# First projections of an encoder layer: spills begun from ScalarE, rows of the first norm stored two tiles later, low parts of those weights on VectorE

## The chip, the core and the metric

The kernel runs on one core of one Trainium2 chip. The core has four compute engines with a queue of instructions each (TensorE, shown as PE; VectorE, DVE; ScalarE, ACT; GpSimd, POOL) and SyncE (SP), which here only starts DMAs. Each queue is worked off in order: an instruction that waits holds up all that stand behind it on its engine. The metric is the device time of one execution in microseconds (us).

## The reference

Two independent sequences of 512 tokens with 1024 features pass through one encoder layer, all in float32. Cut to what matters:

```python
def encoder_layer(x, p, ...):
    h = layer_norm(a * x + 0.5 * swiglu(x, ffn1_wg, ffn1_wu, ffn1_wd), ln1_g, ln1_b)
    proj = h @ w_in
    gq, gk, gv, gr, zf, zb, aq, ak, av = jnp.split(proj, offs, axis=-1)
    o_gla = gla_mixer(gq, gk, gv, gr, zf, zb, ...)   # chunked gated linear attention, both directions
    o_att = gqa_mixer(aq, ak, av, q_norm_g, k_norm_g) # 8 query heads, 2 key heads, 2-D rotary positions
    mix = jnp.concatenate([o_gla, o_att], axis=-1) @ w_out
    h = layer_norm(a * h + mix, ln2_g, ln2_b)
    h = layer_norm(a * h + 0.5 * swiglu(h, ffn2_wg, ffn2_wu, ffn2_wd), ln3_g, ln3_b)
    return h + jax.nn.sigmoid(h @ w_pg + b_pg) * (p @ w_pe)
```

The part of this text is `proj = h @ w_in` and what stands around it: the first norm before it, and attention after it.

## The kernel before

**Numbers in two parts.** TensorE multiplies operands of type fp32r. Each float32 operand is split into a high part, which ScalarE rounds off (line 137), and a low part, the difference, which another engine forms (line 138). Three products (high x high, high x low, low x high) are summed in PSUM. So each piece of weights passes DMA (`raw`, line 149), ScalarE (`w` high), VectorE or GpSimd (`w` low), TensorE. `piece` picks the engine of the low part; for the projections it is GpSimd. `raw` has three buffers, `w` six; a piece is 128x512 (128x288 for the group `akvz`), and a DMA brings two pieces.

**Stages.** Feed-forward layer 1 (0 to about 654 us), the projections and, woven among them, attention and gated linear attention (to about 1200 us), feed-forward layer 2, the gate at the end. This text speaks of the first 110 us of the second stage.

**The first projections.** `projections()` runs groups of matmuls one behind the other: `akvz(0)` (keys, values and decay inputs of sequence 0), `aq(0)` (queries), `g_gr(0)` and `g_gr(1)` (the swish gate of both sequences), then the same for sequence 1, `g_gv` and `g_gqk`. A group (`tok_group`) holds four PSUM banks `pm`, one for each 128 tokens; four steps of two pieces of weights go through all four banks. One tick is three matmuls, a group 32 ticks. A bank is free again when its result is read: ScalarE reads `gr` with Silu into an `ev` buffer (line 757), and since it is needed much later, it is spilled to DRAM (`put`, line 752). `ev` has three buffers, so the fourth result of a group needs the first spill to have landed.

**Side work at ticks.** `main.weave(h1_rows(0), ...)` and its like set side work between ticks: the transposes of the normed rows (`flip`, line 658, in `h1T`), the rows themselves (`h1_rows`: gain and bias on VectorE, lines 650 and 651, then a store `sp_h` of the row tile, 128x1024), and at tick 102 `qk_stacks`, which transposes keys and queries of sequence 0 (line 879, ScalarE lines 884 and 889, VectorE lines 886 and 890). At tick 130 attention begins (line 909 is its first product). The rotary step works on VectorE and GpSimd in turns (lines 807, 812, 814, 815).

**What sets the order.** TensorE's order is the order in which the code is written. The queues of the other engines are ordered by the scheduler of the framework when the program is built. All DMAs go through SP's queue: weights, row stores and spills in one line.

The lines that the change touches, at their places in the listing: `put` (751), `g_gr` (754), `g_gv` (765), `g_gqk` (772), `prefetch` (160), `h1_rows` (1215) and its two weaves (1224, 1226).

Of the kernel before, what the change touches and what calls it, by code (L numbers as in the profile page):

```python
# [20 lines left out]
NT = 4  # L21
# [49 lines left out]
class Layer:  # L71
    def __init__(self, tc, ctx, d, outs):
        self.tc, self.nc, self.d, self.outs = tc, tc.nc, d, outs
        P = lambda name, bufs, **k: ctx.enter_context(tc.tile_pool(name=name, bufs=bufs, **k))
        self.cp = P("const", 1)
        self.xp = P("x", 4)
        self.yp = P("y", 8)
        self.wp = P("w", 6)
        self.rp = P("raw", 3)
        self.rx, self.turn = None, 0  # L80
        self.sp = P("small", 4)
        self.pm = P("pm", 4, space=bass.MemoryType.PSUM)
        self.pd = P("pd", 4, space=bass.MemoryType.PSUM)
        self.X = {}
        self.Y = {}
        self.table = None
        self.queue, self.raws, self.ready = [], [], []
        self.todo, self.W, self.D, self.XB, self.st = [], {}, {}, [], {}

    def const(self, name, shape, dt=F32):  # L90
# [69 lines left out]
    def prefetch(self):  # L160
        while len(self.ready) < 4 and (self.raws or self.queue):
            r = self.raws.pop(0) if self.raws else self.raw(self.queue.pop(0))
            n = r.shape[1] // 2
            self.ready += [self.piece(r[:, :n]), self.piece(r[:, n:])]
        while len(self.raws) < 2 and self.queue:
            self.raws.append(self.raw(self.queue.pop(0)))

# [59 lines left out]
    def load_x(self, X):  # L227
# [20 lines left out]
        def s1(c):  # L248
            sub(raw[0, c], raw[0, c], raw[1, c])
            nc.vector.tensor_tensor(raw[1, c], raw[1, c], raw[1, 2 + c], ALU.add)  # L250
            put(raw[1, c], 4, c)

        def s2(c):
            sub(raw[1, c], raw[1, 2 + c], raw[0, c])
            put(raw[1, c], 5, c)
# [467 lines left out]
class Middle:  # L723
# [24 lines left out]
    def ev(self, name):  # L748
        return self.ep.tile([128, 512], F32, tag="ev", name=name)

    def put(self, n, s, t, tl):
        self.nc.sync.dma_start(self.spill[n, s][t], tl)

    def g_gr(self, s):
        def evac(t, b):
            g = self.ev("gr")
            self.nc.scalar.activation(g, b, AF.Silu)  # L757
            self.put("G", s, t, g)
        return self.L.tok_group(s, 4, 512, 0, evac)

    def preload(self):
# [3 lines left out]
    def g_gv(self, s):  # L765
        def evac(t, b):
            g = self.ev("gv")
            self.nc.scalar.activation(g, b, AF.Copy)
            self.put("gv", s, t, g)
        return self.L.tok_group(s, 4, 512, 0, evac)  # L770

    def g_gqk(self, s):
        nc, L = self.nc, self.L
        for u in range(4):
            w = [L.next_w().rearrange("p h (k f) -> p h k f", k=4) for _ in range(2)]
            p = L.bank_m()
            for kt in range(NKT):
                x = L.X[s][kt // 4][:, kt % 4]
                for m, (a, b) in enumerate(((0, 0), (0, 1), (1, 0))):
                    nc.tensor.matmul(p, w[kt // 4][:, a, kt % 4], x[:, b], start=(kt == 0 and m == 0),  # L780
                                     stop=(kt == NKT - 1 and m == 2))
                if kt == NKT - 1:
                    g = self.ev("gqk")
                    nc.scalar.activation(g, p, AF.Copy, scale=0.125 if u < 2 else 1.0)
                    self.put("gqk", s, u, g)
                yield

    def rms(self, ss, n, div, eps, tag):
# [363 lines left out]
def build(tc, d, outs):  # L1152
    nc = tc.nc
    ctx = ExitStack()
    with ctx:
        L = Layer(tc, ctx, d, outs)
# [10 lines left out]
        h1, z2 = dram("h1"), dram("z2")  # L1167
# [16 lines left out]
        def mid(hp):  # L1184
            L.ident = L.const("ident", (128, 128))
            L.consts(hp)
        with tc.tile_pool(name="rx1", bufs=3, reuse_waits="tile") as L.rx:
            ffn = Ticker(L.ffn(1, lambda s, t: d["x"][s, t * 128:(t + 1) * 128, :], ln_tail(1, L.rx), mid=mid))
            first = L.flip(0, 1, "h1T")
            ffn.put(first, [tail + n for n in (19, 22, 25, 28)])  # L1190
            ffn.end()
        with ExitStack() as mctx:
            M = Middle(L, mctx, h1)
# [16 lines left out]
            main = Ticker(projections())  # L1210
            lnr = M.m8("lnr", (128, 2, 1024))
# [1 line left out]
                L.row(1, j, lnr[:, j])  # L1213

            def h1_rows(s):
                for t in range(NT):
                    L.affine(L.Y[s, t], lnr[:, 0], lnr[:, 1])
                    M.put("h1", s, t, L.Y[s, t])
                    yield
            main.place(first, (1, 5, 9, 13))  # L1220
            main.to(32)
            for _ in L.later:
                pass
            main.weave(h1_rows(0), 4, 48)
            main.weave(L.flip(1, 1, "h1T"), 8, 84)
            main.weave(h1_rows(1), 4, 100)

            main.to(PLAN["s0"])
            main.weave(M.qk_stacks(0, q0, o0[0], (None, 0, 1, 2, 3)), 5, PLAN["s1"])
            main.to(130)  # L1230
            M.preload()
# [56 lines left out]
            main = Ticker(M.wout(1, 0))  # L1288
# [22 lines left out]
        with ExitStack() as fctx:  # L1311
# [38 lines left out]
            main = Ticker(finish())  # L1350
# [93 lines left out]
```

## Time and profile before

| | before |
|---|---|
| median of three runs | 1956.47 us (1953.67 to 1960.98) |
| profiled execution, its own time | 1953.48 us |
| its span, first to last instruction | 1951.7 us |
| TensorE busy | 1877.6 us (96%) |
| VectorE busy | 1413.1 us (72%) |
| ScalarE busy | 873.8 us (45%) |
| GpSimd busy | 860.5 us (44%) |
| mean granted TensorE clock | 0.985 |

The span is what the profile covers; 1.8 us of the execution lie around it. The shares are averages over four stages, so they tell little of one stretch of 110 us: for it the views are asked with a window. In rows of the timeline the first number is the start, the second the time from the first start to the last end of the instructions merged in the row; what stands in brackets is the idle time of the engine before them and what ended it. In rows of waits stand the sum, the count and the longest. In a windows row stand, after the stretch and its length, the busy time (and count) of PE, PEld (weight loads), DVE, ACT and POOL, the granted TensorE clock (1.00 is full speed), the DMA engines' share and GB/s.

### The profile page before, as it was taken

Reading aid. Unit: us, or ns where it says so; the run is one execution under the profiler, and the core shown is the slowest. Engines: PE = TensorE matmul, PEld = TensorE weight load, DVE = VectorE, ACT = ScalarE, POOL = GpSimd, SP = SyncE. Lnnn points to the kernel's source line nnn. Section 1 sums busy time; section 2 is a strip of 40 time slices with the busy share of each in tenths; the row PEclk is TensorE's granted clock in tenths of the full one; section 3 lists DMA queues with packets and bytes.
Section 4 is the critical chain, followed back from the end, with each engine's and each line's share of the span. In section 5 each row is a group of like instructions: output and inputs, shape, how many; then the busy total and the mean of one; then the engine's idle time right before and its main releaser. Section 6 shows DMA issues by size and latency. Waiting matters only on the chain. (4 is left out here: it accounts for less than half of the span.)

```text
span 1951.7 us, 25305 instructions
## 1 busy us (share of the span) xinstructions
PE 1877.6 (96%) x8838; PEld 1535.1 (79%) x8838; DVE 1413.1 (72%) x2143; ACT 873.8 (45%) x1654; POOL 860.5 (44%) x644
## 2 busy tenths in 40 slices
PE   7999999999999898989998898999999999999999
PEld 5788888888888777777876667888888888888787
DVE  7856566666886985788777879556566659895973
ACT  5445544444231355757752437445444442231342
POOL 0665565561550362342233343665565552451243
PEclk9999999999999998999998998999999999999999
DMA  4425443478865224222443231434443479766232
GB/s 180 162 103 173 169 150 144 158 279 343 316 252 195 91 72 156 84 82 92 140 152 87 87 119 55 161 114 158 173 161 141 162 274 338 297 256 247 76 122 84
DMA packets 104959, 322.22 MB, mean 165 GB/s; under 512 B 11008, under 2 KB 38400, under 8 KB 99456
## 3 DMA queue, kind: packets, MB, share of 16 engines
q1 hardware_dynamic: 104832, 320.61, 45.7%
q8 instruction: 70, 1.15, 0.2%
q14 instruction: 57, 0.47, 0.1%
HBM read 218.85 MB, written 101.71 MB: 164 GB/s over the span
## 5 line engine op out<-in xcount | busy, mean ns | idle before, releaser
L138 POOL TENSOR_TENSOR w<-raw,w 128x512 fp32r<-128x512 f32 (+1 forms) x318 | 431.8, 1367 | 750.3 <-ACT w L137 685.6
L137 ACT ACTIVATE w<-raw 128x512 fp32r<-128x512 f32 (+1 forms) x586 | 363.4, 624 | 449.2 <-POOL raw L269 85.8
L269 POOL TENSOR_TENSOR raw<-raw 128x512 f32<-128x512 f32 x240 | 355.9, 1491 | 227.4 <-DVE w L138 155.6
L425 PE MATMUL pm<-X,w 128*128 128x512 f32 x1848 | 434.6, 393 | 10.9 <-ACT X L137 7.8
L425 PEld LDWEIGHTS pm<-X,w 128*128 128x128 f32 x1848 | 347.2, 188 | 89.7 <-ACT X L137 8.6
L138 DVE TENSOR_TENSOR w<-raw,w 128x512 fp32r<-128x512 f32 x268 | 263.2, 990 | 115.5 <-ACT w L137 111.6
L425 PE MATMUL pd<-X,w 128*128 128x512 f32 x1320 | 307.9, 391 | 2.9 <-DVE w L138 2.2
L425 PEld LDWEIGHTS pd<-X,w 128*128 128x128 f32 x1320 | 247.5, 188 | 57.8 <-DVE w L138 3.0
L539 PE MATMUL pm<-w,XB 128*128 128x512 f32 x864 | 198.4, 389 | 0.8 <-DVE Y L523 0.8
L715 PE MATMUL pm<-w,h1T 128*128 128x512 f32 (+1 forms) x768 | 185.6, 384 | 14.0 <-ACT gr L757 9.9
L539 PEld LDWEIGHTS pm<-w,XB 128*128 128x128 f32 x864 | 162.0, 188 | 35.2 <-DVE Y L523 1.7
L138 DVE TENSOR_TENSOR hs<-sg,hs 128x512 fp32r<-128x512 f32 (+1 forms) x182 | 145.4, 818 | 49.6 <-ACT hs L137 48.4
L137 ACT ACTIVATE hs<-sg 128x512 fp32r<-128x512 f32 (+1 forms) x182 | 98.4, 561 | 166.1 <-DVE sg L391 64.8
L715 PEld LDWEIGHTS pm<-w,h1T 128*128 128x128 f32 x768 | 136.3, 195 | 36.5 <-ACT gr L757 10.1
L539 PE MATMUL pd<-w,XB 128*128 128x512 f32 x648 | 148.8, 389 | 0.0
L539 PEld LDWEIGHTS pd<-w,XB 128*128 128x128 f32 x648 | 121.6, 188 | 25.2
L523 DVE TENSOR_TENSOR Y<-Y,pm 128x512 f32<-128x512 f32 x104 | 70.4, 682 | 36.1 <-PE pm L539 36.0
L371 DVE TENSOR_TENSOR sg<-u,pm 128x512 f32<-128x512 f32 x22 | 15.1, 687 | 107.7 <-PE pm L425 107.7
L715 PE MATMUL pm<-w,h3T 128*128 128x512 f32 x384 | 90.6, 393 | 0.0
L715 PEld LDWEIGHTS pm<-w,h3T 128*128 128x128 f32 x384 | 71.2, 188 | 14.7 <-DVE h3T L670 0.2
L660 ACT ACTIVATE pd<-pd,c_lnT 128x512 f32<-128x512 f32 x48 | 36.0, 751 | 92.6 <-PE pd L658 92.6
L523 DVE TENSOR_TENSOR Y<-Y,pd 128x512 f32<-128x512 f32 x88 | 58.7, 678 | 19.3 <-PE pd L539 19.3
(237 smaller groups left out, 2542.1 us busy)
## 6 DMA issues: line engine op xcount, KB each, us to landing
hs<-hs SPq DMA_DIRECT2D x126, 512.0 KB, 2.6
XB<-hs SPq DMA_DIRECT2D x42, 1536.0 KB, 7.0
raw<-in_wgu SPq DMA_DIRECT2D x88, 512.0 KB, 3.4
raw<-in_wd SPq DMA_DIRECT2D x36, 512.0 KB, 7.2
hs_t<-hs SPq DMA_DIRECT2D x56, 256.0 KB, 2.5
XB<-hs_t SPq DMA_DIRECT2D x26, 512.0 KB, 5.1
raw<-in_wout SPq DMA_DIRECT2D x16, 512.0 KB, 3.6
raw<-in_wpg SPq DMA_DIRECT2D x16, 512.0 KB, 3.5
```

Source lines behind the costliest of these rows:

```text
L137: first = nc.scalar.activation(hi, raw, AF.Copy)
L138: (eng or nc.vector).tensor_tensor(lo, raw, hi.bitcast(F32), ALU.subtract)
L269: (sums or self.nc.gpsimd).tensor_tensor(o(), x(), y(), ALU.subtract)
L371: add = lambda o, x, y: nc.vector.tensor_tensor(o, x, y, ALU.add)
L425: nc.tensor.matmul(bank, w[:, a, kt * 128:(kt + 1) * 128], X[k][:, kt, b], start=(k in (0, 1, 4) and kt == 0 and m == 0), stop=(kt == 3 an ...
L523: nc.vector.tensor_tensor(yv, yv, bank, ALU.add)
L539: nc.tensor.matmul(b[t], h[:, a, t * 128:(t + 1) * 128], d[:, c], start=(k in (0, 4, 1) and g == 0 and x == 0), stop=(g == len(H) - 1 and ...
L660: nc.scalar.activation(p, p, AF.Identity, scale=self.lnT[:, c:c + 1], bias=self.lnT[:, c + 8:c + 9])
L715: nc.tensor.matmul(banks[t][:, :width], x[:, i, t * 128:(t + 1) * 128], w[a][:, j], start=(q == 0 and a == 0 and m == 0), stop=(q == nq - ...
```

## The change

1. `put` takes a queue; the spills of `gr`, `gv` and `gqk` (24 DMAs) are issued from ScalarE's queue, behind the activation that writes them. The spills of the decay (`l`, 8) and of the rows (`sp_h`, 8) stay on SP.
2. In `h1_rows` the store of a row tile is written two steps behind its gain and bias; the weave has six steps and ends two ticks (sequence 0) or one tick (sequence 1) later.
3. `piece` gets `eng=self.lows` in `prefetch`. `lows` is VectorE from the start of feed-forward layer 1 until tick 102 of the projections, then None, which means GpSimd as before. Layer 1's own weights don't go through `prefetch`, so this holds for 30 pieces: 8 of 128x288 and 22 of 128x512.

```diff
@@ -85,6 +85,7 @@
         self.Y = {}
         self.table = None
         self.queue, self.raws, self.ready = [], [], []
+        self.lows = None
         self.todo, self.W, self.D, self.XB, self.st = [], {}, {}, [], {}
 
     def const(self, name, shape, dt=F32):
@@ -161,7 +162,7 @@
         while len(self.ready) < 4 and (self.raws or self.queue):
             r = self.raws.pop(0) if self.raws else self.raw(self.queue.pop(0))
             n = r.shape[1] // 2
-            self.ready += [self.piece(r[:, :n]), self.piece(r[:, n:])]
+            self.ready += [self.piece(r[:, :n], eng=self.lows), self.piece(r[:, n:], eng=self.lows)]
         while len(self.raws) < 2 and self.queue:
             self.raws.append(self.raw(self.queue.pop(0)))
 
@@ -748,14 +749,14 @@
     def ev(self, name):
         return self.ep.tile([128, 512], F32, tag="ev", name=name)
 
-    def put(self, n, s, t, tl):
-        self.nc.sync.dma_start(self.spill[n, s][t], tl)
+    def put(self, n, s, t, tl, queue=None):
+        (queue or self.nc.sync).dma_start(self.spill[n, s][t], tl)
 
     def g_gr(self, s):
         def evac(t, b):
             g = self.ev("gr")
             self.nc.scalar.activation(g, b, AF.Silu)
-            self.put("G", s, t, g)
+            self.put("G", s, t, g, self.nc.scalar)
         return self.L.tok_group(s, 4, 512, 0, evac)
 
     def preload(self):
@@ -766,7 +767,7 @@
         def evac(t, b):
             g = self.ev("gv")
             self.nc.scalar.activation(g, b, AF.Copy)
-            self.put("gv", s, t, g)
+            self.put("gv", s, t, g, self.nc.scalar)
         return self.L.tok_group(s, 4, 512, 0, evac)
 
     def g_gqk(self, s):
@@ -782,7 +783,7 @@
                 if kt == NKT - 1:
                     g = self.ev("gqk")
                     nc.scalar.activation(g, p, AF.Copy, scale=0.125 if u < 2 else 1.0)
-                    self.put("gqk", s, u, g)
+                    self.put("gqk", s, u, g, self.nc.scalar)
                 yield
 
     def rms(self, ss, n, div, eps, tag):
@@ -1184,6 +1185,7 @@
         def mid(hp):
             L.ident = L.const("ident", (128, 128))
             L.consts(hp)
+        L.lows = nc.vector
         with tc.tile_pool(name="rx1", bufs=3, reuse_waits="tile") as L.rx:
             ffn = Ticker(L.ffn(1, lambda s, t: d["x"][s, t * 128:(t + 1) * 128, :], ln_tail(1, L.rx), mid=mid))
             first = L.flip(0, 1, "h1T")
@@ -1213,19 +1215,22 @@
                 L.row(1, j, lnr[:, j])
 
             def h1_rows(s):
-                for t in range(NT):
-                    L.affine(L.Y[s, t], lnr[:, 0], lnr[:, 1])
-                    M.put("h1", s, t, L.Y[s, t])
+                for t in range(NT + 2):
+                    if t < NT:
+                        L.affine(L.Y[s, t], lnr[:, 0], lnr[:, 1])
+                    if t >= 2:
+                        M.put("h1", s, t - 2, L.Y[s, t - 2])
                     yield
             main.place(first, (1, 5, 9, 13))
             main.to(32)
             for _ in L.later:
                 pass
-            main.weave(h1_rows(0), 4, 48)
+            main.weave(h1_rows(0), 6, 50)
             main.weave(L.flip(1, 1, "h1T"), 8, 84)
-            main.weave(h1_rows(1), 4, 100)
+            main.weave(h1_rows(1), 6, 101)
 
             main.to(PLAN["s0"])
+            L.lows = None
             main.weave(M.qk_stacks(0, q0, o0[0], (None, 0, 1, 2, 3)), 5, PLAN["s1"])
             main.to(130)
             M.preload()
```

What the framework makes of it is seen in the queues. Line numbers of the changed file lie one to five higher than those before (650 is 651, 651 is 652, 752 is 753, 757 is 758, 829 is 830, 138 is 139). In the names, `Y_3648`, `Y_3659`, `Y_3670` and `Y_3681` are the row tiles of sequence 1, `Y_3529` and `Y_3540` the first two of sequence 0.

**Around the spills of `g_gr(0)`.** SP's queue before, from the last weights of that group on:

```order
L149 DMA raw<-in_wgr 128x1024 x6
L752 DMA sp_h_87<-Y_3648 128x1024
L752 DMA sp_h_88<-Y_3659 128x1024
L752 DMA sp_G_5064<-gr 128x512
L752 DMA sp_G_5065<-gr 128x512
L752 DMA sp_h_89<-Y_3670 128x1024
L752 DMA sp_G_5066<-gr 128x512
```

ScalarE's queue now, at the same place of the program:

```order
L138 ACTIVATE w<-raw 128x512 x2
L758 ACTIVATE gr<-pm 128x512
L753 DMA sp_G_5064<-gr 128x512
L758 ACTIVATE gr<-pm 128x512
L753 DMA sp_G_5065<-gr 128x512
L758 ACTIVATE gr<-pm 128x512
L753 DMA sp_G_5066<-gr 128x512
L758 ACTIVATE gr<-pm 128x512
L138 ACTIVATE w<-raw 128x512
L753 DMA sp_G_5067<-gr 128x512
```

The four spills stood on SP behind the first two row stores of sequence 1; now each stands on ScalarE behind the activation that makes it.

**VectorE before the first key stack** (`K`, which attention needs), before:

```order
L815 TENSOR_TENSOR qr<-qr,sw 128x512 x2
L670 TENSOR_TENSOR h1T_5433<-pd,h1T_5433 128x512
L650 TENSOR_TENSOR Y_3648<-Y_3648,lnr 128x1024
L650 TENSOR_TENSOR Y_3659<-Y_3659,lnr 128x1024
L651 TENSOR_TENSOR Y_3648<-Y_3648,lnr 128x1024
L651 TENSOR_TENSOR Y_3659<-Y_3659,lnr 128x1024
L650 TENSOR_TENSOR Y_3670<-Y_3670,lnr 128x1024
L650 TENSOR_TENSOR Y_3681<-Y_3681,lnr 128x1024
L651 TENSOR_TENSOR Y_3670<-Y_3670,lnr 128x1024
L651 TENSOR_TENSOR Y_3681<-Y_3681,lnr 128x1024
L886 TENSOR_TENSOR K_5824<-pd,K_5824 64x512 x2
```

and now:

```order
L652 TENSOR_TENSOR Y_3659<-Y_3659,lnr 128x1024
L815 TENSOR_TENSOR qr<-qr,c_ropeg 128x512 x2
L816 TENSOR_TENSOR qr<-qr,sw 128x512 x2
L139 TENSOR_TENSOR w<-raw,w 128x512 x2
L652 TENSOR_TENSOR Y_3670<-Y_3670,lnr 128x1024
L651 TENSOR_TENSOR Y_3681<-Y_3681,lnr 128x1024
L139 TENSOR_TENSOR w<-raw,w 128x512
L652 TENSOR_TENSOR Y_3681<-Y_3681,lnr 128x1024
L139 TENSOR_TENSOR w<-raw,w 128x512
L887 TENSOR_TENSOR K_5824<-pd,K_5824 64x512 x2
```

Low parts of weights for the second and third step of `g_gr(1)` now stand behind the rotary step of the queries and among the last row tiles; the first row tiles have moved ahead of that rotary step.

**VectorE before the values** (`V`, whose low part frees the banks of `akvz(0)`), before:

```order
L670 TENSOR_TENSOR h1T_4970<-pd,h1T_4970 128x512
L204 TENSOR_SCALAR lny<-lny 128x4
L650 TENSOR_TENSOR Y_3529<-Y_3529,lnr 128x1024
L647 TENSOR_SCALAR Y_3648<-Y_3648,mv,lny 128x1024
L670 TENSOR_TENSOR h1T_4970<-pd,h1T_4970 128x512
L647 TENSOR_SCALAR Y_3659<-Y_3659,mv,lny 128x1024
L647 TENSOR_SCALAR Y_3670<-Y_3670,mv,lny 128x1024
L647 TENSOR_SCALAR Y_3681<-Y_3681,mv,lny 128x1024
L651 TENSOR_TENSOR Y_3529<-Y_3529,lnr 128x1024
L829 TENSOR_TENSOR V<-pm,V 128x2x64
```

and now:

```order
L651 TENSOR_TENSOR Y_3529<-Y_3529,lnr 128x1024
L204 SCALAR_TENSOR_TENSOR lny<-lna,lny 128x4
L651 TENSOR_TENSOR Y_3540<-Y_3540,lnr 128x1024
L671 TENSOR_TENSOR h1T_4970<-pd,h1T_4970 128x512
L139 TENSOR_TENSOR w<-raw,w 128x512 x2
L202 TENSOR_TENSOR lna<-lny 128x4
L652 TENSOR_TENSOR Y_3529<-Y_3529,lnr 128x1024
L139 TENSOR_TENSOR w<-raw,w 128x512 x2
L830 TENSOR_TENSOR V<-pm,V 128x2x64 x2
```

The four steps of line 647 (the norm of sequence 1) have moved behind the values; four low parts and a further row tile have moved ahead of them.

## The prediction

> **What bounds the kernel now.** TensorE is busy nearly always, so I asked first, for the window 653 to 760 us, which waits TensorE has there:
>
> ```profile
> PE 1877.6 (96%) x8838; PEld 1535.1 (79%) x8838; DVE 1413.1 (72%) x2143; ACT 873.8 (45%) x1654; POOL 860.5 (44%) x644
> PE pm L715 <- ACT gr L757: 9.9, 1, 9.9
> PE pm L715 <- DVE V L829: 4.1, 1, 4.1
> ```
>
> Two, 14.0 us together. The windows around them show what each costs beyond its idle time (the clock is the number before the DMA share):
>
> ```profile
> 668.60:672.70 4.10, 0.01 (x1) 0.00 (x0) 4.10 (x4) 1.79 (x6) 4.10 (x3) 0.87 0.52 179
> 672.70:676.40 3.70, 3.68 (x9) 2.92 (x10) 3.70 (x6) 0.00 (x0) 0.89 (x1) 0.50 0.35 142
> 676.40:680.00 3.60, 3.60 (x13) 2.85 (x12) 3.60 (x7) 0.00 (x0) 0.00 (x0) 0.71 0.81 267
> 727.50:737.40 9.90, 0.06 (x1) 0.00 (x0) 9.90 (x8) 0.63 (x2) 3.49 (x2) 0.61 0.40 159
> 737.40:740.80 3.40, 3.38 (x10) 2.69 (x11) 1.71 (x3) 2.02 (x4) 0.94 (x1) 0.50 1.00 390
> 740.80:744.00 3.20, 3.20 (x13) 2.62 (x12) 1.63 (x3) 2.05 (x4) 1.61 (x2) 0.60 0.96 297
> ```
>
> After each wait the granted clock stays low for some 7 us. The work lost is 3.70 x 0.50 + 3.60 x 0.29 = 2.9 us after the first and 3.40 x 0.50 + 3.20 x 0.40 = 3.0 us after the second. So 4.1 + 2.9 + 9.9 + 3.0 = 19.9 us is what the two waits cost, and the most that their removal can bring. VectorE is busy in all of both idle windows.
>
> The timelines of TensorE, ScalarE and SP show how the long wait arises:
>
> ```profile
> 711.20 15.92 PE L715 MATMUL pm<-w,h1T 128*128 128x512 f32 x69
> 726.96 0.60 PE L879 MATMUL pd<-c_ident,kr 128*128 128x128 f32 x4
> 737.42 2.93 PE L715 MATMUL pm<-w,h1T 128*128 128x512 f32 x6 [9.86 <-ACT gr L757]
> 721.72 0.60 ACT L757 ACTIVATE gr<-pm 128x512 f32<-128x512 f32 x1 [0.76 <-PE pm L715]
> 736.77 0.60 ACT L757 ACTIVATE gr<-pm 128x512 f32<-128x512 f32 x1 [13.00 <-DMA sp_G<-gr]
> 732.10 1.46 SPq L752 DMA_DIRECT2D sp_h<-Y  x2
> 733.61 1.41 SPq L752 DMA_DIRECT2D sp_G<-gr  x2
> L757 ACT ACTIVATE gr<-pm x8: 597/598/600, 719.0 to 760.7; 128x512 f32<-128x512 f32 x8
> ```
>
> The first `gr` result is ready at 719.0 + 0.6 = 719.6; its spill is issued at 733.61, 14.0 us later, right behind two row stores at 732.10. These wait for VectorE. Till the spill lands, the fourth `gr` result has no buffer, its bank isn't freed, and TensorE stands.
>
> VectorE is late because it shares something with GpSimd:
>
> ```profile
> 720.20 10.79 POOL L138 TENSOR_TENSOR w<-raw,w 128x512 fp32r<-128x512 f32 x6
> 725.96 3.91 DVE L650 TENSOR_TENSOR Y<-Y,lnr 128x1024 f32<-128x1024 f32 x2
> 729.79 3.42 DVE L651 TENSOR_TENSOR Y<-Y,lnr 128x1024 f32<-128x1024 f32 x2
> 733.13 2.34 DVE L650 TENSOR_TENSOR Y<-Y,lnr 128x1024 f32<-128x1024 f32 x2
> ```
>
> GpSimd forms low parts until 731.0; in that time a pair of row steps takes 3.91 and 3.42 us, right after it 2.34.
>
> **The change part by part.** *Spills on ScalarE.* The 14.0 us between result and issue go: the issue stands behind the activation on its own queue, and no store is ahead of it. The fourth `gr` then waits only for issue and landing of the first:
>
> ```profile
> L752 SPq DMA_DIRECT2D sp_G<-gr x8: 319/352/909, 733.6 to 761.3; - x8
> DMA to landing us min/median/max: 2.9/3.2/4.3
> ```
>
> 0.35 + 3.2 us against three further results at about 1.37 us each (719.0 to 721.72 is two), so the buffer is back when it is wanted, to within half a microsecond. This wait of 9.9 + 3.0 us goes as far as the spill is its cause. The price is 24 issues on ScalarE, not shown by this trace; by SP's row 24 x 0.35 = 8.4 us, 16 of them (5.6 us) during attention. ScalarE is busy 69% there:
>
> ```profile
> 760.60:1000.00 239.40, 227.19 (x1266) 192.95 (x1265) 185.35 (x360) 165.36 (x365) 75.96 (x69) 0.98 0.30 100
> ```
>
> Behind an issue are queued the softmax exponents and the copies of transposed probabilities, for which VectorE and then TensorE wait. TensorE idles 12.2 of 239.4 us in that stretch, so most of ScalarE's lateness is hidden. Bounds 0 and 5.6 us; I take 0.9, nearer the lower end since ScalarE has 31% free.
>
> The Trainium skill speaks against this part ("DMA: Bandwidth & Descriptors", section "Issuing engines are not separate DMA queues"): DMAs from any engine run on the same 16 engines, and starting them from a second one saves only the time of issuing. By that alone the saving would be a few microseconds. The trace has the 14.0 us not in issuing but in standing in line, so I go by the row; the rule stays as a rival.
>
> *Rows two tiles later.* On SP, weights of `gr` now pass each row store earlier; the stored rows are read back only in `wout`, groups later. Before, no TensorE wait in 653 to 760 us names a DMA of weights. Nothing gained; it hides behind the three `raw` buffers. The woven transposes of sequence 1 move by up to six matmuls (1.4 us), with the banks unchanged: nothing.
>
> *Low parts on VectorE.* Added: 22 pieces of 128x512 and 8 of 128x288, four of which fall into the end of feed-forward layer 1, where VectorE is free a third of the time (27.24 of 40 us busy in the first row). Taken away: what GpSimd holds up.
>
> ```profile
> 600.00:640.00 40.00, 40.00 (x177) 32.77 (x176) 27.24 (x55) 2.42 (x5) 3.15 (x4) 1.00 0.44 159
> L138 DVE TENSOR_TENSOR w<-raw,w x268: 675/694/1824, 5.0 to 1778.4; 128x512 fp32r<-128x512 f32 x134
> 654.16:738.40 84.24, 70.27 (x360) 59.84 (x359) 75.08 (x125) 40.39 (x78) 48.28 (x42) 0.91 0.33 117
> L650 DVE TENSOR_TENSOR Y<-Y,lnr 128x1024 f32<-128x1024 f32 x8 | 12.0, 1516 | 0.0
> L651 DVE TENSOR_TENSOR Y<-Y,lnr 128x1024 f32<-128x1024 f32 x8 | 11.7, 1478 | 0.0
> L647 DVE TENSOR_SCALAR Y<-Y,mv,lny 128x1024 f32<-128x1024 f32 x4 | 6.3, 1624 | 0.0
> L647 DVE TENSOR_SCALAR Y<-Y,mv,lny x8: 805/995/1785, 639.4 to 668.5; 128x1024 f32<-128x1024 f32 x8
> L650 DVE TENSOR_TENSOR Y<-Y,lnr x8: 1207/1216/2278, 662.3 to 734.3; 128x1024 f32<-128x1024 f32 x8
> L814 DVE TENSOR_TENSOR qr<-qr,c_ropeg 128x512 f32<-128x512 f32 x4 | 6.0, 1498 | 2.7 <-POOL sw L812 2.7
> L815 DVE TENSOR_TENSOR qr<-qr,sw 128x512 f32<-128x512 f32 x4 | 5.3, 1352 | 0.0
> ```
>
> From the end of layer 1 to the first key stack VectorE is busy 75.1 of 84.2 us. Added: 22 x 0.69 = 15.2, and four of 288 at 0.44 (0.69 by size, with a fixed part: an estimate) = 1.8; 17.0. Removed: rows at their shortest, 1.207, 0.805 and (size and kind as the low part) 0.69: 8 x 0.31 + 8 x 0.27 + 4 x 0.82 = 7.9, and 4 x 0.81 + 4 x 0.66 = 5.9 in the rotary step; 13.8, and smaller steps not counted. From 7.9 (the rotary step stays, since GpSimd's own half of it runs on) to some 20 us. I take 16: VectorE needs 75.1 + 17.0 - 16 = 76 us, as much as before. But TensorE is earlier: without the first wait it is at the key transposes at 727.0 - 6.5 = 720.5. VectorE comes to its key rows at 654.2 + 76 = 730 without any idle time, at 739 with the 9.2 us of before; part of that was spent on work that TensorE paced and that now comes earlier, so I take a third, 733. Ahead of the key rows, by the order shown, are two row steps of line 651, one of 650 and the last two low parts: 3 x 1.2 + 2 x 0.7 = 5.0 us, so weights of the second step of `g_gr(1)` are ready at 728. TensorE wants them two ticks and some transposes after 720.5: at 722.5. **The wait moves: 5.5 us for low parts from VectorE**, or in part for a bank that the key rows (line 886) free late. With a low clock after it (2.9 and 3.0 us above), 5.5 + 2.5 = 8.0 us; bounds 0 (VectorE keeps up) and 739 - 5 - 722.5 + 3 = 14.5.
>
> The first wait, for `V`: its row stood behind four norm steps and two row steps,
>
> ```profile
> 665.71 4.55 DVE L647 TENSOR_SCALAR Y<-Y,mv,lny 128x1024 f32<-128x1024 f32 x3
> 670.18 2.28 DVE L651 TENSOR_TENSOR Y<-Y,lnr 128x1024 f32<-128x1024 f32 x1
> 672.39 0.28 DVE L829 TENSOR_TENSOR V<-pm,V 128x128 fp32r<-128x128 f32 x1
> ```
>
> and now has ahead of it from 662 on three row steps, one `h1T` and four low parts: 3 x 1.2 + 0.7 + 4 x 0.7 = 7.1, so 669 for 672.4, against TensorE's 668.6. I keep 0.5 us of the 4.1 + 2.9 = 7.0; bounds 0 and 7.0. That is the 6.5 us used above.
>
> **Sum:** 1953.5 (the profiled execution) - 19.9 + 0.5 + 8.0 + 0.9 = **1943.0**. The median of the runs lies 3.0 above that execution, with 7.3 us between lowest and highest; for the median I say 1944.
>
> The Trainium skill ("TensorE: Matmul & The Clock Gate", section "What's actually happening") has the clock fall after an idle window of about 3.4 us. By that rule waits that are each shorter would cost no clock, and the sum would be 2.5 us less. A wait of 2.6 us in this trace was followed by 0.61:
>
> ```profile
> 794.60:797.20 2.60, 0.01 (x1) 0.01 (x1) 2.44 (x4) 0.63 (x2) 0.80 (x1) 1.00 0.26 74
> 797.20:800.60 3.40, 3.38 (x10) 2.57 (x11) 2.82 (x6) 2.87 (x7) 0.00 (x0) 0.61 0.24 98
> ```
>
> so I leave the clock's share in.
>
> **Rivals.** *VectorE keeps up.* The low parts fall into its idle 9.2 us; no wait is left. For it: its demand is no larger than before. Against: its waits in that stretch are for the rotary halves and for ScalarE, which remain. 1953.5 - 19.9 + 0.9 = 1934.5, with leftovers to 1939.
>
> *VectorE becomes the bound outright.* A low part stands in line for its high part, which waits for TensorE to release a buffer; VectorE then idles at places where GpSimd did so for nothing. At the upper bounds, 1953.5 - 19.9 + 0.5 + 14.5 + 5.6 = 1954.2; 1949 to 1956.
>
> *Slower.* The slow VectorE rows are not due to GpSimd. Then 17 us are added and nothing is removed: key rows at 738.5 + 17 = 755.5 (749 if counted from the 733 above); the weights 5 us ahead, at 750.5, for 722.5. TensorE waits 28 us and 3 for the clock: 1953.5 - 19.9 + 0.5 + 31 + 0.9 = 1966. Worse than before it is as soon as less than some 6 us are removed. Against it: 3.42 beside GpSimd and 2.34 after it, for the same kind of row.
>
> *The change does not do what it says.* Only SP's issuing is saved, 8 x 0.35 = 2.8 us, since the spill's landing is what was late: 1950.7. That is the time by the skill's rule on issuing engines. Against it: landings of 3.2 us beside 14.0 in line.
>
> **How the numbers follow.** Forecast (1940 to 1949) 0.56; VectorE keeps up 0.17; VectorE the bound 0.17; slower 0.05; only issuing 0.05. The range 1935 to 1955 takes in the second and third cases nearly whole and leaves out some 0.15. What a measurement tells from no change is about 0.5%, 9.8 us: below 1946.7 is faster. Of the forecast 0.41 lies there, with the second case's 0.17: 0.58. The rest of the forecast, the third and the last: 0.37, of which 0.01 I give to slower, with the fourth: 0.06.
>
> **What would show it.** Attention's first product stood here:
>
> ```profile
> 760.62 0.62 PE L909 MATMUL pd<-K,Q 128*128 128x512 f32 x2
> ```
>
> Right: it comes at 760.6 - 19.9 + 0.5 + 8.0 = 749 (746 to 755); TensorE's wait for `gr` is gone or under 1 us, `sp_G` issued within 1 us of its activation; lines 650 and 651 near 1.21 us on VectorE; a new TensorE wait after 715 us that names VectorE's low parts or key rows. Wrong: that product before 744 (VectorE kept up) or after 756 (it did not), or TensorE waits on ScalarE from there to the end of attention that sum to over 6 us.

## The result

| | before | after |
|---|---|---|
| median | 1953.95 us (8 runs, 1947.80 to 1960.98) | 1937.78 us (8 runs, 1935.03 to 1946.96) |
| span of the profiled execution | 1951.7 us | 1933.4 us |
| mean granted clock in it | 0.985 | 0.992 |

The ratio is 0.9924, with a 95% interval of 0.9903 to 0.9944: some 15 us faster. Run again beside the last experiments, on a chip where the kernel before had a median of 1950.84 (22 runs), the changed kernel took 1938.39 (12 runs), ratio 0.9937 (0.9917 to 0.9956).

The spans differ by 18.3 us. Four marks on TensorE divide it: the first product of the projections, attention's first product (line 909 before, 910 after), the first transposes of the gated linear attention (1030, 1031), and the wait at the second norm.

| stretch | before | after | gain |
|---|---|---|---|
| layer 1 | 653.80 | 655.63 | -1.8 |
| **first projections, up to attention's first product** | **106.82** | **94.35** | **12.5** |
| attention | 252.06 | 249.67 | 2.4 |
| gated linear attention | 183.97 | 178.79 | 5.2 |
| the rest | 755.05 | 754.96 | 0.1 |

The change's own stretch gave 12.5 us. Layer 1 and the gated linear attention are not its work: of layer 1's 1.8 us one window of low clock at 66 us makes 1.7, which the profile before doesn't have, and the gated linear attention has nearly the same waits in both; the last section shows that such lengths differ all the same. Of attention's 2.4 us a part is the change's, as all profiles together show (under e6). I therefore judge every experiment by the first projections' stretch, which the second profile of the changed kernel repeats at 94.36, and by the median beside it.

### The profile page after: what moved, and what is told of

Same layout as the page of the kernel before. It is cut to its first block, busy times and chain, and to the rows that moved or that the text cites. A ratio compares the mean times of both kernels' runs of the same rounds, so it can differ in the third digit from the quotient of the medians.

```text
span 1933.4 us, 25273 instructions
## 1 busy us (share of the span) xinstructions
PE 1867.3 (97%) x8838; PEld 1529.5 (79%) x8838; DVE 1406.2 (73%) x2173; ACT 874.0 (45%) x1654; POOL 822.3 (43%) x614
## 5 line engine op out<-in xcount | busy, mean ns | idle before, releaser
L139 POOL TENSOR_TENSOR w<-raw,w 128x512 fp32r<-128x512 f32 (+1 forms) x288 | 391.5, 1367 | 651.6 <-ACT w L138 602.0
L139 DVE TENSOR_TENSOR w<-raw,w 128x512 fp32r<-128x512 f32 (+1 forms) x298 | 281.9, 954 | 117.2 <-ACT w L138 113.2
L716 PE MATMUL pm<-w,h1T 128*128 128x512 f32 (+1 forms) x768 | 180.2, 377 | 0.0
```

Source lines behind the costliest of these rows:

```text
L139: (eng or nc.vector).tensor_tensor(lo, raw, hi.bitcast(F32), ALU.subtract)
L716: nc.tensor.matmul(banks[t][:, :width], x[:, i, t * 128:(t + 1) * 128], w[a][:, j], start=(q == 0 and a == 0 and m == 0), stop=(q == nq - ...
```

## The profile after

The engines' busy times on the page of the changed kernel:

```profile
PE 1867.3 (97%) x8838; PEld 1529.5 (79%) x8838; DVE 1406.2 (73%) x2173; ACT 874.0 (45%) x1654; POOL 822.3 (43%) x614
```

and the waits of TensorE in 653 to 760 us (sum, count, longest):

```profile
PE pd L880 <- DVE K L887: 6.0, 1, 6.0
```

Both old waits (9.9 for `gr`, 4.1 for `V`) are gone. One is left, in their place: for a bank `pd` that VectorE's key rows free. Its cost, from the windows (the clock stands before the DMA share):

```profile
655.63:730.87 75.24, 73.38 (x397) 62.95 (x395) 69.64 (x151) 41.56 (x81) 15.43 (x18) 1.00 0.42 144
728.90:735.05 6.15, 0.11 (x1) 0.03 (x1) 4.83 (x8) 2.74 (x5) 0.00 (x0) 0.68 0.52 181
735.05:738.50 3.45, 3.45 (x11) 2.91 (x12) 3.42 (x6) 2.72 (x7) 0.03 (x1) 0.57 0.00 0
```

6.05 us of waiting and 3.45 x 0.43 = 1.5 us of low clock. The first row ends where the key rows begin: VectorE has been busy 69.6 us by then, against 75.4 before, although it forms the low parts now; GpSimd fell from 48.3 to 15.4.

The timelines of TensorE, ScalarE and VectorE around the wait:

```profile
721.52 0.60 PE L880 MATMUL pd<-c_ident,kr 128*128 128x128 f32 x4
735.05 1.08 PE L880 MATMUL pd<-c_ident,qr 128*128 128x128 f32 x4 [6.05 <-DVE K L887]
749.98 0.63 PE L910 MATMUL pd<-K,Q 128*128 128x512 f32 x2
713.55 0.60 ACT L758 ACTIVATE gr<-pm 128x512 f32<-128x512 f32 x1 [0.73 <-PE pm L716]
714.18 0.35 ACTq L753 DMA_DIRECT2D sp_G<-gr  x1
732.28 1.20 ACT L885 ACTIVATE K<-pd 64x512 fp32r<-64x512 f32 x2 [7.75 <-DVE K L887]
...
714.30 1.22 DVE L651 TENSOR_TENSOR Y<-Y,lnr 128x1024 f32<-128x1024 f32 x1
715.44 1.29 DVE L808 TENSOR_TENSOR qr<-qr,qk0y 128x512 f32<-128x512 f32 x2
722.86 1.29 DVE L139 TENSOR_TENSOR w<-raw,w 128x512 fp32r<-128x512 f32 x2
724.07 1.22 DVE L652 TENSOR_TENSOR Y<-Y,lnr 128x1024 f32<-128x1024 f32 x1
725.20 2.30 DVE L651 TENSOR_TENSOR Y<-Y,lnr 128x1024 f32<-128x1024 f32 x1
727.43 1.78 DVE L139 TENSOR_TENSOR w<-raw,w 128x512 fp32r<-128x512 f32 x1
730.87 1.37 DVE L887 TENSOR_TENSOR K<-pd,K 64x512 fp32r<-64x512 f32 x2
733.51 1.40 DVE L887 TENSOR_TENSOR K<-pd,K 64x512 fp32r<-64x512 f32 x2 [1.26 <-ACT K L885]
```

The spill is issued 0.03 us after its activation instead of 14.0 us. The two low parts of the second step of `g_gr(1)` are ready at 723.5 and 724.1; TensorE begins that step at 723.7, and no wait names them. What is late is the key rows: ScalarE needs VectorE's first pair before it copies the second half, and the bank is free only after VectorE's second pair, at 734.9.

## The experiments

"Stretch" is the time from the first product of the projections to attention's first product: 106.82 before, 94.35 after.

**Each part alone.** e1 is the `put` part of the diff above without the rest, e2 the `h1_rows` part with its two weaves, e3 the `lows` part (the assignment at layer 1, its end at tick 102, and `eng=self.lows`).

> Part 1 alone: all 24 spills of gr, gv and gqk are issued from ScalarE; the row stores stand as before and the low parts stay on GpSimd. My theory (three separate faults: the spill in line on SP, V's row late on a VectorE that GpSimd slows, key rows late on VectorE): TensorE's wait for gr is under 1.5 us instead of 9.9; the wait for V stays at 4.1; VectorE's rows L650 and L651 stay near 1.5 us in the mean; since TensorE now comes to the key transposes at 727 while VectorE still ends its rows at 737.7, a new wait for a bank that the key rows (L886) free appears, of 7.3 us (737.7 + 4 for the two pairs of key rows and ScalarE's copies between them, against 727.0 + 7.4). Profiled execution 1953.5 - 9.9 - 3.0 + 7.3 + 2 = 1950. Rival (the line on SP was the only fault): no wait names the key rows, 1953.5 - 12.9 + 0.9 = 1941.5.

> Part 2 alone: row stores two steps later; spills on SP, low parts on GpSimd. In SP's order one row store instead of two then stands ahead of the first gr spill. My theory: the store of that first row of sequence 1 still waits for VectorE (about 731.5 in the profile before), so the first spill is issued near 732 instead of 733.6, the wait for gr shrinks by at most 2 us to about 8, the wait for V stays at 4.1, and the time is 1951 to 1953.5. Rival (the distance between a row and its store was the fault): the wait for gr falls below 3 us and the time to 1943.

> Part 3 alone: low parts of those weights on VectorE; all spills on SP behind two row stores, as before. My theory: the rows of sequence 1 are done earlier on a VectorE that GpSimd doesn't slow, so the row stores ahead of the spill go at about 713 and 718 instead of 732; the first gr spill is issued near 718.3, some 3 us behind its result, the wait for gr is 1.5 to 3 us, the wait for V is 0, and the wait for the bank of the key rows is 4 to 6 us. L650 and L651 (here L651 and L652) near 1.25 us. Profiled execution 1938 to 1942: most of the gain without any change of queue. Rival (the queue is what matters): the wait for gr stays near 9.9, 1953.5 - 7.0 = 1946.5 or more. Rival (VectorE gets more work and is the bound): the waits in 655 to 760 sum to 14 us or more, 1953.

| | stretch | median | ratio to before |
|---|---|---|---|
| e1, spills | 102.31 | 1946.38 | 0.9976 (0.9957 to 0.9994) |
| e2, rows | 104.81 | 1951.36 | 0.9996 (0.9976 to 1.0016) |
| e3, low parts | 92.94 | 1938.94 | 0.9925 (0.9901 to 0.9949) |

TensorE's waits in that stretch in e1:

```profile
PE pd L879 <- DVE K L886: 7.4, 1, 7.4
PE pm L715 <- DVE V L829: 4.1, 1, 4.1
```

in e2:

```profile
PE pm L715 <- ACT gr L757: 7.9, 1, 7.9
PE pm L715 <- DVE V L829: 4.1, 1, 4.1
PE pm L715 <- POOL w L138: 0.7, 1, 0.7
```

and in e3:

```profile
PE pd L880 <- DVE K L887: 3.4, 1, 3.4
```

**The low parts alone bring 13.9 us in the stretch, more than the full change; the spills alone 4.5, the rows alone 2.0.** With spills alone the wait for `gr` is gone, and TensorE runs into the same late VectorE 7 us further on, as the first theory said (7.3 us); the time is some 4 us less than the 1950 forecast. ScalarE's queue can stand as well. The fourth `gr` of e1 is written at 726.7, and its spill is issued ten microseconds later, by the profile when a row store of SP had landed:

```profile
736.75 0.33 ACTq L752 DMA_DIRECT2D sp_G<-gr  x1
737.13 0.63 ACT L137 ACTIVATE w<-raw 128x512 fp32r<-128x512 f32 x1 [9.95 <-DMA sp_h<-Y]
```

No wait of TensorE names this, since VectorE's first key row came later still, at 740.7. In the full change, where the rows are in time, the same spill is issued at once. What ties it to the store I have not followed.

With the low parts alone the wait for `gr` is gone too, and the spills are still on SP behind two row stores. The timelines of SP and ScalarE in e3 show how:

```profile
712.77 3.88 SPq L753 DMA_DIRECT2D sp_h<-Y  x2
716.75 1.90 SPq L753 DMA_DIRECT2D sp_G<-gr  x3
713.59 0.60 ACT L758 ACTIVATE gr<-pm 128x512 f32<-128x512 f32 x1 [0.72 <-PE pm L716]
719.73 0.60 ACT L758 ACTIVATE gr<-pm 128x512 f32<-128x512 f32 x1 [1.43 <-DMA sp_G<-gr]
```

The row stores go at 712.8 and about 716.3 instead of 732.1 and 733.2, since the rows are ready; the first spill waits 2.6 us in line, ScalarE 1.43 us for a buffer, and TensorE not at all. I had expected 1.5 to 3 us of TensorE's time there, and 4 to 6 us for the bank, which took 3.4.

**GpSimd's share.** In e5 the 30 low parts are formed nowhere (`half` holds for the pieces of `prefetch` until tick 102, `low` is 0 for them and 1 for all others):

```diff
-        hi = self.split(src, w[:, 0, :n], w[:, 1, :n], eng or self.nc.gpsimd)
+        if half:
+            hi = self.nc.scalar.activation(w[:, 0, :n], src, AF.Copy).ins
+            self.half.append(w)
...
-                        nc.tensor.matmul(banks[t][:, :width], x[:, i, t * 128:(t + 1) * 128], w[a][:, j],
+                        nc.tensor.matmul(banks[t][:, :width], x[:, i, t * 128:(t + 1) * 128], w[a][:, j * low[a]],
```

> The kernel before, with the 30 low parts of the first projections left out on every engine (TensorE multiplies by the high part a second time in their place, so its work is the same; the output lacks those terms). Spills on SP and row stores as before. It takes away what GpSimd does beside VectorE and adds nothing to VectorE. My theory (GpSimd's low parts made VectorE slow): L650 and L651 fall from 1.5 to 1.22 us and L647 from 1.62 to 0.81; the wait for V is 0; the row stores ahead of the spill go before 717, so the wait for gr is under 3 us with the queue unchanged; the wait for the bank of the key rows is under 1 us. Profiled execution 1933 to 1938. Against e3_lows (spans 1937.5, bank wait 3.4) the difference is the price of the 17 us of low parts on VectorE: some 3 to 5 us. Rival (VectorE is slow by itself): rows stay near 1.5 us, waits of 4 and 8 to 10 us stay, 1950 or more.

Stretch 87.38, median 1933.18. The spills are on SP here, behind the row stores, and the waits of 9.9 and 4.1 us are gone all the same, without a bank wait in their place. TensorE's only wait in 653 to 752 us:

```profile
PE pm L722 <- ACT gr L764: 0.4, 1, 0.4
```

The rows on VectorE in e1, where GpSimd forms the low parts (busy time, mean ns of one):

```profile
L650 DVE TENSOR_TENSOR Y<-Y,lnr 128x1024 f32<-128x1024 f32 x8 | 12.0, 1520 | 0.0
L647 DVE TENSOR_SCALAR Y<-Y,mv,lny 128x1024 f32<-128x1024 f32 x8 | 9.3, 1217 | 0.0
```

and the same steps in e5, five lines further down in its listing:

```profile
L655 DVE TENSOR_TENSOR Y<-Y,lnr 128x1024 f32<-128x1024 f32 x8 | 9.6, 1218 | 0.0
L652 DVE TENSOR_SCALAR Y<-Y,mv,lny 128x1024 f32<-128x1024 f32 x8 | 6.1, 811 | 0.0
```

The windows from the first product of the projections to VectorE's first key row (the third busy time is VectorE's, the fifth GpSimd's), before:

```profile
653.80:738.47 84.67, 70.70 (x364) 60.23 (x363) 75.44 (x125) 40.80 (x79) 48.28 (x42) 0.91 0.33 117
```

in e5:

```profile
657.40:725.36 67.96, 67.54 (x366) 58.23 (x365) 55.53 (x126) 40.75 (x80) 9.74 (x16) 1.00 0.42 146
```

and in e3:

```profile
655.65:728.25 72.60, 72.60 (x395) 62.64 (x394) 67.55 (x152) 42.05 (x81) 15.00 (x17) 1.00 0.43 150
```

VectorE's busy time up to the key rows is 75.4 us beside GpSimd's low parts (before), 55.5 without them, and 67.6 when it forms them itself. So GpSimd's low parts cost VectorE 19.9 us; the same work costs 12.0 on VectorE. Against e3 the stretch is 5.6 us shorter: that is what the added work still costs, 3.0 us of it in waits of TensorE and nearly all of the rest in the low clock after e3's wait. The Trainium skill ("SBUF — State Buffer", section "Who interferes with whom") says that an instruction of VectorE with two SBUF inputs and one of GpSimd that reads SBUF exclude each other, so that the later one stands until the other is done. The rows agree that they hold each other up: line 650 falls from 1.52 to 1.22 us. Which of the two stands is another matter (e4). Line 647, with one input of that size, falls too, from 1.22 to 0.81 us.

**The row stores.** e4 is the change without its second part.

> Parts 1 and 3, without the rows two tiles later. My theory: the row delay is worth nothing, since no wait of TensorE names weights of gr: no wait for gr or V, a wait of about 6 us for the bank of the key rows, profiled execution within 2 us of the full change's 1935. Rival (the delay keeps weights of gr from standing behind row stores): a wait for low parts or high parts of w after 690 us of over 2 us, 1938 or more.

Stretch 91.88, median 1936.46, ratio 0.9916 (0.9889 to 0.9942): 2.5 us shorter in the stretch than the full change. The wait for the bank is 3.4 us instead of 6.0. The profiled execution was 1942.38, not the 1935 I expected; the gated linear attention took 188.1 us in it, longer than in any other profile. VectorE's timeline in e4:

```profile
712.88 1.28 DVE L808 TENSOR_TENSOR qr<-qr,qk0y 128x512 f32<-128x512 f32 x2
720.30 1.29 DVE L139 TENSOR_TENSOR w<-raw,w 128x512 fp32r<-128x512 f32 x2
721.51 2.35 DVE L651 TENSOR_TENSOR Y<-Y,lnr 128x1024 f32<-128x1024 f32 x2
723.78 2.35 DVE L652 TENSOR_TENSOR Y<-Y,lnr 128x1024 f32<-128x1024 f32 x2
726.05 1.29 DVE L139 TENSOR_TENSOR w<-raw,w 128x512 fp32r<-128x512 f32 x2
727.25 1.37 DVE L887 TENSOR_TENSOR K<-pd,K 64x512 fp32r<-64x512 f32 x2
```

GpSimd's two low parts at that time (shortest, median and longest in ns, first and last start), in e4 and then in the full change:

```profile
L139 POOL TENSOR_TENSOR w<-raw,w x2: 1258/3290/5322, 723.2 to 728.4; 128x512 fp32r<-128x512 f32 x2
L139 POOL TENSOR_TENSOR w<-raw,w x2: 2278/2310/2342, 724.1 to 726.4; 128x512 fp32r<-128x512 f32 x2
```

The key transposes stand at 720.59 here and at 721.52 in the full change, so the queries' scaling (line 808) comes 7.7 us ahead of them here and 6.1 us there. Six steps up to tick 101 write the four rows at ticks 84, 86, 89 and 92, where four steps up to tick 100 write them at 84, 88, 92 and 96: only the stores come later, the rows themselves earlier. So one more row step of 1.22 us (at 714.30 in the full change) lies ahead of line 808, and one fewer behind it, which by itself is no loss. Yet the way from line 808 to the key rows is not shorter in the full change but 1.1 us longer (15.43 against 14.37). There GpSimd's first two low parts of its own fall together with VectorE's steps in both kernels. In the full change both lose, in turns: VectorE's steps take 2.30 and 1.78 us where they take 1.22 and 0.68 elsewhere in its timeline, GpSimd's 2.34 and 2.28. In e4 VectorE loses nothing, and GpSimd's first low part takes 5.32 us, the second 1.26. VectorE's loss of 2.2 us is most of the 2.7 us by which the bank wait is longer. Why VectorE loses in one order and not in the other, I have not tested.

**Issues on ScalarE during attention.** e6 puts `gv` and `gqk` back on SP:

```diff
-            self.put("gv", s, t, g, self.nc.scalar)
+            self.put("gv", s, t, g)
-                    self.put("gqk", s, u, g, self.nc.scalar)
+                    self.put("gqk", s, u, g)
```

> The full change, but only the 8 spills of gr are issued from ScalarE; the 16 of gv and gqk go back to SP. It measures the price of 16 issues on ScalarE during attention. My theory: they cost at most 1 us, as ScalarE has 31% free there; TensorE's waits between 770 and 1000 stay within 1 us of those of the full change, and the profiled execution within 3 us of 1935. Rival (each issue delays softmax by its 0.33 us): 4 to 5.6 us faster than the full change, 1930.

Median 1941.79, above the 1932 to 1938 that I expected; ratio 0.9951 (0.9934 to 0.9968), whose interval overlaps with those of the full change. TensorE's waits in 755 to 990 us sum to 12.2 us, against 12.1 in the full change and 12.2 before: the 16 issues cost nothing that shows, and taking them off ScalarE gains nothing. The stretch is 95.03.

The profiles of all 14 runs together show that these issues even gain a little. Attention, from its first product to the first transposes of the gated linear attention, took 249.67 to 251.48 us in the eight kernels that issue the 16 spills from ScalarE, and 251.55 to 252.69 us in the six that leave them on SP; the means lie 1.7 us apart. In each of the six TensorE waits 0.94 to 1.12 us some 126 us into attention, and in none of the eight. In the kernel before:

```profile
886.75 0.63 PE L923 MATMUL pd<-c_ident,P 128*128 128x128 f32 x4 [0.94 <-DVE sm L916]
```

Whether the queue does this or the changed order of ScalarE's instructions is not shown.

**Is it the bank?** e7 spreads the transposes of the stacks; e8 does the same without the second part:

```diff
-            s1=112,
+            s1=127,
```

> The full change, with the transposes of keys and queries spread over 25 ticks instead of 10 (102 to 127). If the wait of 6.0 us that is left in the full change is for a bank that the key rows free late on VectorE, then TensorE wants that bank 8.2 us later and waits 0; no low clock follows; attention's first product comes at 743 instead of 750 and the time is 7 us less: 1928 in the profile, 1930.5 in the median. Rival (low parts from VectorE are what is late): the wait stays near 6 us, under another name, and so does the time. Rival (attention then waits for its queries instead): a new wait of up to 6 us at attention's first product, 1935.

> Parts 1 and 3 without the rows two tiles later, and the transposes spread over 25 ticks as in e7. The bank wait of 3.4 us in e4 goes to 0, attention's first product comes at 743, as in e7, since TensorE then waits for nothing from 655 us on: median 1930 to 1932, the same as e7 within 2 us. If part 2 has a worth of its own (weights passing row stores), this run shows a wait for w that e7 has not.

e7: stretch 87.83, 6.5 us less than the full change, and median 1935.10, ratio 0.9917 (0.9896 to 0.9939), 4.6 us over the forecast of 1930.5. e8: stretch 86.72, median 1930.91, ratio 0.9899 (0.9876 to 0.9922). TensorE's waits in 653 to 760 us in e7 (the two of `P` and `sm` belong to attention):

```profile
PE pd L924 <- DVE P L918: 1.6, 1, 1.6
PE pm L716 <- ACT gr L758: 1.3, 2, 0.9
PE pd L924 <- DVE sm L917: 0.8, 1, 0.8
```

and in e8:

```profile
PE pd L924 <- DVE P L918: 1.6, 1, 1.6
```

The bank wait is gone in both, and no wait for low parts takes its place: it was the bank. Attention's first product comes at 745.20 and 741.90, and e8's median lies 4.2 us below e7's, where I had expected 2 at most. In e7 a little comes back, 0.4 us of the wait for `gr` ahead of that product and 0.9 behind it: `gr` activations now stand on ScalarE behind copies of queries that VectorE lets go late.

**What is needed of the three parts?** The last four ran on one chip. e9 is e1 with `s1=127`, e10 is e3 with it, e11 is the kernel of e8, e12 the full change.

> Part 1 and the transposes over 25 ticks; low parts stay on GpSimd, rows as before. It asks whether the low parts have to move at all once the two waits that the spills and the key rows make are gone by other means. Stretch from the first projection's first product to attention's first product: 106.8 us in the profile before, 102.3 with part 1 alone, 91.9 with parts 1 and 3, 86.7 with the late transposes too. If it is enough that nobody waits for a slow VectorE: the bank wait of 7.4 us and its clock (some 2) go, the wait for V of 4.1 us (and its clock) stays, stretch 92 to 94, median 1937 to 1940. If the slow VectorE is late for whatever comes next: a new wait of 3 us or more for queries or rows after 735 us, stretch 97 or more, 1943.

> Part 3 and the transposes over 25 ticks; all spills on SP, rows as before. It asks what part 1 is worth when VectorE is in time. In e3 the stretch was 92.9 us against 91.9 with part 1. Theory now (VectorE's lateness was behind both old waits, and the queue of the spills mattered only since the row stores ahead of them waited for VectorE): stretch 87 to 89 us, median within 2 us of e8's 1930.9. Rival (the spills need their own queue): a wait for gr of over 3 us, stretch over 90, 1935.

> The kernel of e8 again, beside the full change and the two above on one chip: median 1929 to 1933, 5 to 8 us less than the full change; stretch 86.5 to 87.5.

> The full change again on this chip: median 1936 to 1940; stretch 94 to 95.5, wait for the bank of the key rows 6.0. What lies behind attention differs from run to run by the clock alone: the transposes of the gated linear attention have the same waits, 1.2 to 3.1 us, in every profile, and low clock follows some of them in one run and others in the next.

| | stretch | median | ratio to before |
|---|---|---|---|
| e9, spills, stacks late | 95.47 | 1939.32 | 0.9951 (0.9933 to 0.9968) |
| e10, low parts, stacks late | 86.76 | 1934.12 | 0.9918 (0.9893 to 0.9943) |
| e11, both, stacks late | 86.70 | 1931.56 | 0.9902 (0.9873 to 0.9930) |
| e12, full change | 94.36 | 1938.39 | 0.9937 (0.9917 to 0.9956) |

With the low parts on VectorE the queue of the spills is worth 0.06 us of the stretch. With the stacks early e4 is 1.06 us shorter than e3, but not by the queue: the bank wait is the same (3.37 and 3.42 us), and the difference is the low clock after it. The 5.57 us behind the wait in e3, then in e4:

```profile
732.44:738.01 5.57, 5.57 (x15) 4.52 (x16) 4.85 (x8) 3.74 (x7) 1.58 (x2) 0.50 0.08 31
731.43:737.00 5.57, 5.56 (x20) 4.62 (x21) 4.84 (x8) 3.75 (x8) 1.58 (x2) 0.69 0.05 19
```

That is 5.57 x 0.50 = 2.8 us of work lost against 5.57 x 0.31 = 1.7. Without the low parts on VectorE, the late stacks bring e9 to 95.5, between the two forecasts (92 to 94, and 97 or more), with 4.1 us for `V`, 1.4 for `gr` and 0.5 for a low part left in the stretch. The best kernel found, parts 1 and 3 with late stacks, takes 19 us less than before in its median (1931.56 against 1950.84) and 7 us less than the full change on the same chip, in the stretch 7.7; the intervals of these two overlap by a little. Part 1 might be left out of it: e10's median is 3.2 us above that of e8, where I had allowed 2, and 2.6 above that of e11, which these intervals don't tell from nothing, though its attention is longer by as much (252.69 us against 250.04).

## Why the prediction was right or wrong

1944 was forecast, 1935 to 1955 as its range; 1937.8 and 1938.4 were measured. Faster was the likelier side, and it is faster; the inner range of 1940 to 1949, which had the largest chance, was missed.

*The two old waits (19.9 us).* Right: both are gone. The 0.5 us kept for `V` wasn't there: nothing.

*The new wait (8.0 us).* Its size was near, 6.05 + 1.5 = 7.5, and attention's first product came at 750.0, forecast 749. Its cause was half wrong. The step that failed is the time of the low parts ahead of the key rows: I put them at 728 and let TensorE wait for them from 722.5; the second was ready at 724.1, although layer 1 ended 1.8 us later than before, and what TensorE waited for was the bank, the half I had only mentioned. e7 shows it.

*What VectorE is spared (16 us).* Too small: 19.9 by e5. And the low parts cost 12.0 instead of 17.0. Their durations in e3 do sum to 16.9 us, but each begins some 0.08 us before the step ahead of it ends (two in a row took 1.29), and so does the step behind it; in e3 VectorE's steps up to the key rows overlap by 10.0 us in all, in e5 by 5.3. The key rows came at 730.9; I had 733.

*The wait for `gr` is the spill's.* Here the explanation failed, though the sum didn't show it. I took 9.9 + 3.0 us for part 1's gain, "as far as the spill is its cause". The runs say that VectorE's lateness was behind it: with the low parts moved, the spill may stay in line on SP (e3), and with the spill moved alone the lateness comes back as a bank wait of 7.4 us (e1). The line on SP was only the way in which a slow VectorE reached TensorE. I had seen that the row stores wait for VectorE, and had not asked whether they would still be late after part 3.

*Rows two tiles later (nothing).* Wrong: it costs 2.5 us beside the other two parts (e4), 1.1 with the stacks late (e7 against e8), and gains 2.0 alone (e2). I looked at the stores and overlooked that six steps in the place of four write the rows earlier; in the order that came of it VectorE lost 2.2 us to GpSimd.

*Issues on ScalarE (0.9 us).* Of the wrong sign: no cost shows (e6), and attention is some 1.7 us shorter where they stand on ScalarE.

*The rivals.* That only issuing is saved (1950.7 for the whole change) was nearer to the truth about part 1 than I allowed: alone it brought 4.5 us of the stretch, and beside part 3 0.06. The Trainium skill ("DMA: Bandwidth & Descriptors", section "Issuing engines are not separate DMA queues") has a second issuing engine save only the time of issuing; with VectorE in time the runs agree for this stretch. "VectorE keeps up" (1934.5 to 1939) holds the measured time, yet by luck and not by its own step, since VectorE did not keep up; 7.5 us remained. The slower case rested on GpSimd being innocent, which e5 rules out.

*The rest.* My sum gains 11.4 us in the stretch, measured 12.5. Beyond that the forecast stood on a median of three runs, 1956.47; more runs of the kernel before have their median at 1950.8 to 1954.0. And the profiled execution after, 1935.2, lies 7.8 us below the sum's 1943.0: 1.1 us of that come from the stretch, 3.3 from attention (a loss of 0.9 forecast, a gain of 2.4 measured), and 5.2 from the gated linear attention, which no part of the change explains and which I call luck; layer 1 took 1.8 back.

## What to carry to other kernels

When several waits in a stretch go back to one late engine, changing the way in which its lateness reaches the bottleneck moves the wait on by a few microseconds; taking work off that engine, or the contention that slows it, removes them together (3.4 us of waiting were left with the low parts moved, 0.4 with them left out). An engine's busy time can be inflated by another's work: compare the same instruction's duration with and without it before deciding that the engine has no room. And read a change of a weave by the ticks at which each piece is now written, not by what the piece is meant to delay.

## What the runs showed of the hardware

**The clock falls by windows, and equal waits do not cost the same.** Every low stretch in the 14 profiles inside the span lasts 3.41 us or a multiple of it (3.41, 6.83, 10.24, 13.65), and within one profile all begin on one grid of 3.413 us. I cut each profile into such windows and took those that run at full clock and in which TensorE stands for over 0.5 us. Of 234 with less than 1.1 us idle none was followed by a low window; of 140 with 1.1 to 1.9 us, 30; of 77 with 1.9 us or more, all. (The first 11 to 18 us of each span, ahead of the first record of the clock, are left out.) So a wait of 2 us costs clock when it falls into one window, and may cost none when it is shared by two. Between 1.1 and 1.9 us the idle time alone does not decide. One and the same wait of the gated linear attention (1.8 us for `W`) lies whole within one window both before and after, and only before is the next window low. The kernel before:

```profile
1052.00:1054.00 2.00, 0.18 (x3) 0.20 (x3) 1.84 (x6) 0.00 (x0) 0.17 (x1) 0.99 1.01 259
1054.00:1056.00 2.00, 2.00 (x7) 1.28 (x6) 1.97 (x5) 0.60 (x1) 1.93 (x2) 0.50 0.27 102
```

and in the changed one:

```profile
1038.90:1040.80 1.90, 0.09 (x2) 0.06 (x1) 1.74 (x6) 0.00 (x0) 0.03 (x1) 1.00 1.01 235
1040.80:1042.80 2.00, 2.00 (x19) 1.53 (x21) 1.97 (x4) 0.60 (x1) 1.93 (x2) 1.00 0.40 154
```

In e8 a wait of 1.3 us, up to 1040.73, was followed by 13.7 us at half clock:

```profile
1042.50:1056.20 13.70, 13.70 (x52) 9.40 (x52) 4.67 (x16) 2.56 (x8) 2.95 (x2) 0.50 0.27 78
```

The gated linear attention, with a dozen such waits, took 178.8 to 188.1 us in the 14 profiles, whatever the kernel; the 5.2 us between before and after lie within that. The Trainium skill ("TensorE: Matmul & The Clock Gate", section "What's actually happening") has a free-running window of 3413 ns, and the grid agrees; it has the clock fall after an idle window, while here 1.9 us of idleness in one sufficed each time. What decides in a window with 1.1 to 1.9 us of idleness, and why a low stretch lasts up to four windows with TensorE busy, stays open.

**VectorE and GpSimd hold each other up, on either side.** A low part of GpSimd took 5.32 us in e4, and 1.26 right after, while VectorE ran its steps at their shortest (1.22 and 0.68 us), four of which began after it. In the full change both lost: VectorE's single steps took 2.30 and 1.78 us while GpSimd's low parts took 2.34 and 2.28. So by the profile's start times it was not always the one that began first that went on. Over the whole stretch the work moved off GpSimd sped VectorE up by more than it cost there: 19.9 us against 12.0.
